# Letting two token ranges take turns by single matmuls, by threes and by twos in three of a down projection's seven products

## The chip, the cores and the metric

One core of one Trainium2 chip runs the kernel. The metric is the device time of one execution in microseconds (us). Before the change three executions took 1509.31, 1510.66 and 1514.90 us; the median is 1510.66 us. One execution was also taken with the hardware profiler, and its trace is what the views below are made of.

## The reference, cut to what matters

The kernel computes one layer of a hybrid decoder for 1024 prompt tokens and 64 sample tokens. The change lies in the last matrix product of the feed-forward part, the down projection `(gelu(a) * b) @ w_down`, with 2816 rows of weights and 1024 columns:

```python
def conv_ffn(h, w_up, conv_w, conv_b, w_down, prev):
    z = h @ w_up
    ...
    a, b = jnp.split(c, 2, axis=-1)
    return (jax.nn.gelu(a) * b) @ w_down, zp[:, T:]

def layer(...):
    ...
    f, nconv = conv_ffn(rmsnorm(x, norm_ffn), w_up, conv_w, conv_b, w_down, conv_prev)
    return x + f, nk, nv, nconv, vn
```

After it come only the residual addition and the final RMSNorm. The values are float32; the kernel reaches that accuracy with matmuls on rounded operands: each operand is split into a high part and a low part (`wh`, `wl` for weights, `th`, `tl` for tokens), and a product is the sum of three matmuls, `wh*th + wh*tl + wl*th`.

## The kernel before, in words

The down phase is the last stage. It multiplies 2x2 blocks by a scheme with seven products in place of eight. `DN_ORDER = (5, 0, 2, 4, 6, 1, 3)` is the order in which the products run; `at` counts them from 0. Each product has 11 units (`NU`), a unit being 128 rows of the contraction. A unit has its weights, 4 blocks `m` of 128 columns, and its tokens, 544 of them. The 544 tokens are two ranges `e`: a **wide** one of 288 tokens (`e == 0`) and a **narrow** one of 256 (`e == 1`).

`mm_dn(m, e, i, ws, new)` issues the three matmuls of one block and one range. The stationary operand is the block of weights, the moving operand is the range of tokens, and the output goes to `place(m, e)`: six PSUM banks (`dn`) hold the results, one bank for each of the four wide outputs, and two narrow outputs together in each of the other two banks (m = 0, 1 and m = 2, 3). So a unit is 4 x 2 x 3 = 24 matmuls, 12 wide and 12 narrow, and a product is 264. Every matmul brings its own weight load (LDWEIGHTS) along.

The loop over blocks of units: the first two and the last two units of a product go together, in two halves of two `m` each (`mp`); the seven between go one at a time with all four `m`. Within each the range `e` is the outer loop, then the units `x`, then `m`, then the three matmuls. So a single unit issues its 12 wide matmuls and then its 12 narrow ones.

When the last two units of a product are done, `take` adds each of the eight outputs from PSUM to the residual tile `x` in SBUF on VectorE (DVE, L1750). The next product may write to a bank only when that bank's takes are done. A first write with `start` clears the whole bank, and only the products at 0, 1 and 5 start anew; the others go on adding.

The operands are made ahead: SyncE (SP) issues the loads of raw weights (`wraw`, `a`) and raw tokens (`traw`); ScalarE (ACT) rounds to the high part (L40), DVE subtracts to get the low part (L41), and in some products DVE also adds two blocks of weights first (L443, L447). `units` asks for weights two units ahead and tokens some units ahead. The instructions go to the engines' queues in an order that the framework's scheduler makes of the program; the kernel has no table of times.

Of the kernel before, what the change touches and what calls it, by code (L numbers as in the profile page):

```python
# [34 lines left out]
def layer(tc, a):  # L35
# [11 lines left out]
    with ExitStack() as top:  # L47
# [310 lines left out]
        with ExitStack() as ph1:  # L358
# [98 lines left out]

            for j in DN_ORDER:
                for i in range(NFF // 2):
# [530 lines left out]
            for at, (pair, gs, whole) in enumerate(seq):  # L990
# [16 lines left out]
                ws, to = [], W.used + 7  # L1007
# [518 lines left out]
        def t_upto(loads, splits):  # L1526

            for n in range(len(ts["raw"]), min(loads, 7 * (NFF // 2))):
                j, i = DN_ORDER[n // (NFF // 2)], n % (NFF // 2)
                raw = dnp["t"].tile([P, 576], F32, name="traw", bufs=4)[:, :HT]  # L1530
                nc.sync.dma_start(raw, td[i][:, T_AT[j]])
                ts["raw"].append(raw)
# [185 lines left out]
        with ExitStack() as ph3:  # L1718
            def pool3(name, bufs, **kw):
                return ph3.enter_context(tc.tile_pool(name=name, bufs=bufs, reuse_waits="tile", **kw))  # L1720
# [4 lines left out]
            def x_load(dh, th):  # L1725
                x = x1[dh, th] = xp.tile([P, 4, HT], F32, name=f"x{dh}{th}")
                for m in range(4):
                    nc.sync.dma_start(x[:, m], x1d[4 * dh + m][:, HT * th:HT * th + HT])
# [3 lines left out]
            def place(m, e):  # L1732
                b = bank[m] if e == 0 else bank[4 + m // 2]
                return b[:, 0:288] if e == 0 else b[:, 256 * (m % 2):256 * (m % 2) + 256]

            def mm_dn(m, e, i, ws, new):
                (wh, wl), (th, tl) = ws
                lo, hi = spans[e]
                for k, (u, v) in enumerate(((wh, th), (wh, tl), (wl, th))):
                    PE.matmul(place(m, e), u[:, m, :], v[:, lo:hi],  # L1740
                              start=new and i + k == 0 and (e == 0 or m % 2 == 0),
                              stop=i == NU - 1 and k == 2, skip_group_check=True)

            def take(j, m, e):

                dh, th, op = {5: (0, 0, V.tensor_add), 0: (0, 0, V.tensor_add), 2: (0, 1, V.tensor_add),
                              4: (1, 1, V.tensor_sub), 6: (1, 0, V.tensor_sub), 1: (1, 1, V.tensor_sub),
                              3: (0, 1, V.tensor_add)}[j]
                x = x1[dh, th][:, m, spans[e][0]:spans[e][1]]
                return op(x, x, place(m, e))  # L1750
# [77 lines left out]
            def units(n, count):  # L1828
                out = []
                for x in range(n, n + count):  # L1830
                    t_upto(x + 5, x + 3)
                    w = W.get(2, 3)
                    out.append((w, ts["made"][x]))
                return out
# [17 lines left out]

            for at, j in enumerate(DN_ORDER):
                new, last, n0 = j in (5, 0, 1), at == 6, at * NU
                blocks = [(0, 2), *((x, x + 1) for x in range(2, NU - 4 if last else NU - 2))]
                if not last:
                    blocks.append((NU - 2, NU))
                for lo, hi in blocks:
                    if at == 0:
                        if lo in (2, 5):  # L1860
                            later.pop(0)()
                        if lo == 8:
                            nc.sync.dma_start(a["tails"], stc)
                            ph2.close()
                            own["s2"], own["a22"] = pool3("s2", 1), pool3("a22", 1)
                            xp, lp = pool3("xp", 1), pool3("lp", 1)
                            acc += [lp.tile([P, HT], F32, name=f"acc{th}") for th in range(2)]
                            x_load(0, 0)
                    for go in hooks.get((at, lo), ()):
                        go()  # L1870
                    got = units(n0 + lo, hi - lo)
                    for mp in range(2) if hi - lo == 2 else (0,):
                        for e in range(2):
                            for x in range(lo, hi):
                                for m in range(2 * mp, 2 * mp + 2) if hi - lo == 2 else range(4):
                                    mm_dn(m, e, x, got[x - lo], new)
                        if hi == NU:
                            for m in (2 * mp, 2 * mp + 1):
                                for e in range(2):
                                    take(j, m, e)  # L1880
            got = units(7 * NU - 4, 4)
            for e in range(2):
                sqs = []
                for m in range(4):
                    for x in range(4):
                        mm_dn(m, e, NU - 4 + x, got[x], False)
                    if e and m == 0:
                        last_scale(0, range(4))
                        fin[2] = fin_rms(1, 0, last)
                    elif e and m == 1:  # L1890
                        rb = fin_rb(*fin[2])
                        last_mul(0, 0, rb, 0, 4)
                    for m in (m - 1, m) if m % 2 and e else () if e else (m,):
                        taken = take(3, m, e)
                        sqs.append(square(0, 1, m, e, False, m < 3 - e))
                    if e and m == 1:
                        last_scale(1, (0, 1))
                last = sqs[3 - e:]
# [14 lines left out]

NSTG, FEW, NPRE = 4, 3, 2
DN_ORDER = (5, 0, 2, 4, 6, 1, 3)
T_AT = {5: 0, 3: 1, 0: 2, 4: 3, 1: 4, 2: 5, 6: 6}
OUTS = dict(y=(KD, P, T), kp=(P, 2, P), vp=(P, 256), ksn=(P, 2, NS), vsn=(8, 8, 256),
            ks=(8, 120, 256), vso=(8, 120, 256), tails=(P, 44, 9, 2), gvs=(NS, GW))
# [82 lines left out]
```

## Time and profile before

| | |
|---|---|
| three executions | 1509.31, 1510.66, 1514.90 us; median 1510.66 us |
| the profiled execution, its own time | 1509.93 us |
| its span, first to last instruction | 1508.2 us |
| granted TensorE clock, mean | 0.998 |
| DVE busy | 1158.7 us (77%) |
| ACT busy | 825.9 us (55%) |
| POOL busy | 265.8 us (18%) |
| DMA | 286.70 MB, mean 190 GB/s |

Engines: PE is TensorE's matmuls, PEld its weight loads, which run beside the matmuls; DVE is VectorE, ACT is ScalarE, POOL is GpSimd, SP is SyncE. In the timeline a row is: start in us, duration in us, engine, line, operation, output and inputs by the program's names, shape, count, and in brackets the idle time before it with what ended it. A matmul's duration overlaps with the next matmuls; what a matmul costs in a stream is the distance from its start to the next start, called its **pitch** here. The table of windows gives the busy time and number of instructions of each engine in a stretch, then the granted clock, the share of the DMA engines that was busy, and GB/s.

### The profile page before, as it was taken

Reading aid. Unit: us, or ns where it says so; the run is one execution under the profiler, and the core shown is the slowest. Engines: PE = TensorE matmul, PEld = TensorE weight load, DVE = VectorE, ACT = ScalarE, POOL = GpSimd, SP = SyncE. Lnnn points to the kernel's source line nnn. Section 1 sums busy time; section 2 is a strip of 40 time slices with the busy share of each in tenths; the row PEclk is TensorE's granted clock in tenths of the full one; section 3 lists DMA queues with packets and bytes.
Section 4 is the critical chain, followed back from the end, with each engine's and each line's share of the span. In section 5 each row is a group of like instructions: output and inputs, shape, how many; then the busy total and the mean of one; then the engine's idle time right before and its main releaser. Section 6 shows DMA issues by size and latency. Waiting matters only on the chain.

```text
span 1508.2 us, 31375 instructions
## 1 busy us (share of the span) xinstructions
PE 1493.7 (99%) x12190; PEld 1481.7 (98%) x12190; DVE 1158.7 (77%) x1909; ACT 825.9 (55%) x1755; POOL 265.8 (18%) x422
## 2 busy tenths in 40 slices
PE   9999999999999999999999999999999999999997
PEld 9999999999999999999999999999999999999997
DVE  6896778756645995989668888898899888785685
ACT  6665764544543774874434555555555556453463
POOL 0000012200120331530222322322132122000002
PEclk9999999999999999999999999999999999999999
DMA  8452457637749757849978333332233226973453
GB/s 289 157 188 112 179 177 265 228 126 271 243 167 333 249 181 224 254 160 322 342 257 282 129 115 122 117 117 107 98 136 109 91 74 219 367 259 97 123 183 133
DMA packets 137508, 286.70 MB, mean 190 GB/s; under 512 B 15248, under 2 KB 44368, under 8 KB 137360
## 3 DMA queue, kind: packets, MB, share of 16 engines
q1 hardware_dynamic: 132352, 279.97, 55.2%
q10 hardware_dynamic: 5008, 4.73, 0.9%
q8 instruction: 96, 1.57, 0.4%
q14 instruction: 52, 0.43, 0.1%
HBM read 195.76 MB, written 90.85 MB: 190 GB/s over the span
## 4 chain that ended last, share of the span: by engine, by line
PE 76%; DVE 5%; ACT 2%; issue 1%; DMA 1%; POOL 0%; DVEq 0%; ACTq 0%; POOLq 0%
PE st L300 41%; PE dn L1740 15%; PE mm L240 14%; PE sc L1233 1%; PE mx L841 1%; PE po L1294 1%; ACT s L1256 1%; DVE s L1259 1%; DVE s L1243 1%; DVE nm L1249 1%; PE pt L1266 1%; DVE of L1305 0%; DVE wl L41 0%; DVE pl L41 0%; DMA v<-gvd 0%
## 5 line engine op out<-in xcount | busy, mean ns | idle before, releaser
L300 PE MATMUL st<-th,wh 128*128 128x256 f32 (+1 forms) x2128 | 610.6, 287 | 1.2 <-ACT ku L283 0.8
L300 PE MATMUL st<-tl,wh 128*128 128x256 f32 (+1 forms) x2128 | 608.7, 286 | 0.0
L300 PE MATMUL st<-th,wl 128*128 128x256 f32 (+1 forms) x2128 | 608.2, 286 | 0.0
L300 PEld LDWEIGHTS st<-th,wh 128*128 128x128 f32 x2128 | 399.9, 188 | 2.6 <-ACT k L281 1.2
L300 PEld LDWEIGHTS st<-th,wl 128*128 128x128 f32 x2128 | 400.3, 188 | 0.0
L300 PEld LDWEIGHTS st<-tl,wh 128*128 128x128 f32 x2128 | 399.7, 188 | 0.0
L40 ACT CAST wh<-wraw 128x512 fp32r<-128x512 f32 (+2 forms) x204 | 139.4, 694 | 99.7 <-PE st L300 35.3
L41 DVE TENSOR_TENSOR wl<-wraw,wh 128x512 fp32r<-128x512 f32 (+2 forms) x204 | 158.5, 790 | 40.2 <-ACT wh L40 38.3
L1740 PE MATMUL dn<-th,wh 128*128 128x288 f32 (+1 forms) x616 | 176.7, 287 | 0.0
L1740 PE MATMUL dn<-tl,wh 128*128 128x288 f32 (+1 forms) x616 | 176.2, 286 | 0.0
L1740 PE MATMUL dn<-th,wl 128*128 128x288 f32 (+1 forms) x616 | 175.1, 284 | 0.0
L40 ACT CAST wh<-ws 128x512 fp32r<-128x512 f32 x160 | 98.1, 622 | 99.8 <-PE st L300 65.5
L41 DVE TENSOR_TENSOR wl<-ws,wh 128x512 fp32r<-128x512 f32 x160 | 111.1, 707 | 44.1 <-ACT wh L40 42.1
L1740 PEld LDWEIGHTS dn<-th,wl 128*128 128x128 f32 x616 | 115.8, 188 | 0.0
L1740 PEld LDWEIGHTS dn<-tl,wh 128*128 128x128 f32 x616 | 115.7, 188 | 0.0
L1740 PEld LDWEIGHTS dn<-th,wh 128*128 128x128 f32 x616 | 115.6, 188 | 0.0
L288 POOL TENSOR_TENSOR z<-ku,k 128x256 f32<-128x256 f32 (+1 forms) x32 | 29.5, 926 | 316.7 <-ACT ku L283 315.4
L41 DVE TENSOR_TENSOR tl<-traw,th 128x544 fp32r<-128x544 f32 (+1 forms) x85 | 61.4, 730 | 22.9 <-ACT th L40 22.8
L40 ACT CAST th<-traw 128x544 fp32r<-128x544 f32 (+1 forms) x85 | 53.8, 642 | 43.9 <-PE dn L1740 28.6
L240 PE MATMUL mm<-s,wh 128*128 128x256 f32 (+1 forms) x384 | 76.7, 294 | 0.0
L531 PE MATMUL st<-w2h,th 128*128 128x256 f32 x308 | 74.5, 283 | 0.2 <-DVE w2l L165 0.2
L240 PE MATMUL mm<-oh,wh 128*128 128x256 f32 (+1 forms) x256 | 73.5, 288 | 0.2
(300 smaller groups left out, 3157.9 us busy)
## 6 DMA issues: line engine op xcount, KB each, us to landing
wraw<-wt SPq DMA_DIRECT2D x133, 512.0 KB
traw<-td SPq DMA_DIRECT2D x77, 272.0 KB
td<-za SPq DMA_DIRECT2D x22, 544.0 KB
wraw<-wt SPq DMA_DIRECT2D x35, 256.0 KB
upd<-hl SPq DMA_DIRECT2D x14, 512.0 KB
td<-t SPq DMA_DIRECT2D x11, 544.0 KB
qd<-q SPq DMA_DIRECT2D x8, 576.0 KB
q<-qd SPq DMA_DIRECT2D x8, 576.0 KB
```

Of the source, the lines that this page charges most:

```text
L40: S.copy(hi, src)
L41: V.tensor_sub(lo, src, hi.bitcast(F32))
L240: PE.matmul(ps[:, lo:lo + c1 - c0], u[:, k, :], v[:, c0:c1], start=(clear and k == 0 and i == 0), stop=(k == nk - 1 and i == 2), skip_grou ...
L288: op(to, pick(x, to, lo, hi), pick(y, to, lo, hi))
L300: PE.matmul(ps, u[:, kk, :], v, start=first and kk + i == 0, stop=kk == 3 and i == 2, skip_group_check=True)
L531: PE.matmul(ps, u, v[:, k, :], start=k + i == 0, stop=k == KD - 1 and i == 2)
L841: PE.matmul(ps[:, P * i:P * i + P], vn[:, i], late["wst"][:, c, :], start=True, stop=True)
L1233: PE.matmul(ps[:, h, o0:256], q, kst[kv][:, e, k0:cur + P], start=e == 0, stop=e == 1)
L1243: V.copy_predicated(s[:, :, 0:P], late["mprev"].to_broadcast([P, 4, P]), ps[:, :, 0:P])
L1249: V.tensor_reduce(nm, s, AX.X, ALU.max, negate=True)
L1256: S.activation(s[:, h], s[:, h], AF.Exp, bias=nm[:, h:h + 1], accum_out=dn[:, h:h + 1])
L1740: PE.matmul(place(m, e), u[:, m, :], v[:, lo:hi], start=new and i + k == 0 and (e == 0 or m % 2 == 0), stop=i == NU - 1 and k == 2, skip_g ...
```

## The change

A table `TURNS` says for the products at 1, 2 and 3 how the two ranges take turns; the other four products are as before. `mm_dn` gets an argument `ks`, the subset of its three matmuls to issue.

```diff
-            def mm_dn(m, e, i, ws, new):
+            def mm_dn(m, e, i, ws, new, ks=range(3)):
                 (wh, wl), (th, tl) = ws
                 lo, hi = spans[e]
                 for k, (u, v) in enumerate(((wh, th), (wh, tl), (wl, th))):
+                    if k not in ks:
+                        continue
                     PE.matmul(place(m, e), u[:, m, :], v[:, lo:hi],
...
                     for mp in range(2) if hi - lo == 2 else (0,):
-                        for e in range(2):
+                        turn = TURNS.get(at)
+                        for e in range(1 if turn else 2):
                             for x in range(lo, hi):
                                 for m in range(2 * mp, 2 * mp + 2) if hi - lo == 2 else range(4):
-                                    mm_dn(m, e, x, got[x - lo], new)
+                                    for k, d in turn or ((range(3), e),):
+                                        mm_dn(m, d, x, got[x - lo], new, k)
...
+TURNS = {1: [((k,), e) for k in range(3) for e in range(2)],
+         2: [(range(3), e) for e in range(2)],
+         3: [((k,), e ^ (k % 2)) for k in range(3) for e in range(2)]}
```

The same 264 matmuls run in each product, each with its own weight load; only their order differs. With W for a wide matmul and N for a narrow one, a block `m` of a unit now reads W N W N W N at 1 (singles), W W W N N N at 2 (threes), and W N N W W N at 3 (twos, with a single at each end). Within a product the order goes from wide to narrow 11 times before, and 132, 44 and 88 times now; consecutive matmuls write to different banks 61 times before, and 263, 87 and 175 times now.

TensorE, the first matmuls of the product at 1, before (names with their numbers: `dn_16951` and `dn_16952` are the wide outputs of m = 0 and 1, `dn_16955` the bank of the narrow outputs of m = 0 and 1, `th_17339` the first unit's tokens and `th_17351` the second's; in brackets the engines whose semaphore the instruction waits for):

```order
L1740 MATMUL dn_16951<-th_17339,wh_17309 128x288 [waits DVE_49,Activation_49]
L1740 MATMUL dn_16951<-tl_17340,wh_17309 128x288
L1740 MATMUL dn_16951<-th_17339,wl_17310 128x288
L1740 MATMUL dn_16952<-th_17339,wh_17309 128x288 [waits DVE_49]
L1740 MATMUL dn_16952<-tl_17340,wh_17309 128x288
L1740 MATMUL dn_16952<-th_17339,wl_17310 128x288
L1740 MATMUL dn_16951<-th_17351,wh_17357 128x288 [waits Activation_49]
L1740 MATMUL dn_16951<-tl_17352,wh_17357 128x288
L1740 MATMUL dn_16951<-th_17351,wl_17358 128x288
L1740 MATMUL dn_16952<-th_17351,wh_17357 128x288
L1740 MATMUL dn_16952<-tl_17352,wh_17357 128x288
L1740 MATMUL dn_16952<-th_17351,wl_17358 128x288
```

The same place with the change:

```order
L1742 MATMUL dn_16951<-th_17339,wh_17309 128x288 [waits DVE_49,Activation_49]
L1742 MATMUL dn_16955<-th_17339,wh_17309 128x256 [waits DVE_49]
L1742 MATMUL dn_16951<-tl_17340,wh_17309 128x288
L1742 MATMUL dn_16955<-tl_17340,wh_17309 128x256
L1742 MATMUL dn_16951<-th_17339,wl_17310 128x288
L1742 MATMUL dn_16955<-th_17339,wl_17310 128x256
L1742 MATMUL dn_16952<-th_17339,wh_17309 128x288
L1742 MATMUL dn_16955<-th_17339,wh_17309 128x256
```

The first narrow matmul, with its wait for DVE's takes out of the shared bank `dn_16955`, was the 13th matmul of the product and is now the second; the second unit's weights and tokens were first needed at the 7th matmul and are now first needed at the 13th.

VectorE, the end of the product at 1, as a piece of the difference (L1750 and L1752 are `take`; L447 adds weights for a later unit, L41 makes low parts):

```order
 L41 TENSOR_TENSOR tl<-traw,th 128x544
-L1750 TENSOR_TENSOR x_17296<-x_17296,dn 128x288 x2
+L447 TENSOR_TENSOR s_17922<-s_17501,a_17858 128x512
+L1752 TENSOR_TENSOR x_17296<-x_17296,dn 128x288
 L41 TENSOR_TENSOR wl<-s_17860,wh 128x512
-L1750 TENSOR_TENSOR x_17296<-x_17296,dn 128x256 x2
-L447 TENSOR_TENSOR s_17922<-s_17501,a_17858 128x512
-L1750 TENSOR_TENSOR x_17296<-x_17296,dn 128x288 x2
+L1752 TENSOR_TENSOR x_17296<-x_17296,dn 128x256
+L1752 TENSOR_TENSOR x_17296<-x_17296,dn 128x288
+L1752 TENSOR_TENSOR x_17296<-x_17296,dn 128x256
```

The addition for a later unit now stands ahead of the takes, and the takes of the wide and narrow outputs alternate. SyncE's order is the same but for line numbers; ACT's order differs in a few neighbouring rounding and squaring steps.

## The prediction

> **What bounds the kernel now.** The page comes first: how busy each engine is, and the granted clock in 40 slices. Then the end of the chain of waits in order of time (start, us, what).
>
> ```profile
> span 1508.2 us, 31375 instructions
> ...
> PE 1493.7 (99%) x12190; PEld 1481.7 (98%) x12190; DVE 1158.7 (77%) x1909; ACT 825.9 (55%) x1755; POOL 265.8 (18%) x422
> ...
> PEclk9999999999999999999999999999999999999999
> ```
>
> ```profile
> 1267.10 185.64 PE dn L1740 x1512
> ```
>
> TensorE is busy nearly all the time at full clock, and the chain runs through the matmuls of the down phase in one piece of 185.64 us. A time on PE there is a time of the kernel. Next the table of windows, one window for each of the products at 1, 2, 3 and, for comparison, 4 (length, busy PE, PEld, DVE, ACT and POOL with counts, clock, DMA share, GB/s):
>
> ```profile
> 1299.35:1331.77 32.42, 32.42 (x267) 32.42 (x265) 27.95 (x50) 16.67 (x30) 0.00 (x0) 1.00 0.96 346
> 1331.77:1364.18 32.41, 32.41 (x266) 32.41 (x265) 25.84 (x48) 14.53 (x29) 0.00 (x0) 1.00 0.66 212
> 1364.18:1396.59 32.41, 32.41 (x266) 32.41 (x265) 17.93 (x31) 13.06 (x24) 0.00 (x0) 1.00 0.33 96
> 1396.59:1429.01 32.42, 32.42 (x267) 32.42 (x265) 20.80 (x37) 14.33 (x28) 0.00 (x0) 1.00 0.46 136
> ```
>
> The products take 32.41 to 32.42 us each although DVE, ACT and the DMA engines are very differently loaded in them (DMA from 0.33 to 0.96). So nothing but PE's own stream sets their length, and the reader should ask what sets the stream's pitch. The timeline of PE at the start of the product at 1 answers that.
>
> ```profile
> 1299.24 0.28 PE L1740 MATMUL dn<-th,wl 128*128 128x256 f32 x1
> 1299.35 0.29 PE L1740 MATMUL dn<-th,wh 128*128 128x288 f32 x1
> 1299.49 0.30 PE L1740 MATMUL dn<-tl,wh 128*128 128x288 f32 x1
> ...
> 1300.81 0.29 PE L1740 MATMUL dn<-th,wl 128*128 128x288 f32 x1
> 1300.94 0.28 PE L1740 MATMUL dn<-th,wh 128*128 128x256 f32 x1
> 1301.05 0.28 PE L1740 MATMUL dn<-tl,wh 128*128 128x256 f32 x1
> ...
> 1302.19 0.28 PE L1740 MATMUL dn<-th,wl 128*128 128x256 f32 x1
> 1302.30 0.29 PE L1740 MATMUL dn<-th,wh 128*128 128x288 f32 x1
> 1302.43 0.30 PE L1740 MATMUL dn<-tl,wh 128*128 128x288 f32 x1
> ```
>
> Twelve wide matmuls go from 1299.35 to 1300.94: 1.59 us, a pitch of 132.5 ns. Twelve narrow ones go from 1300.94 to 1302.30: 1.36 us, 113.3 ns. Together 2.95 us, and 11 units of that are 32.45 us, the product's length to 0.04 us. There is no gap left to remove.
>
> **The change, part by part.** Nothing is added or taken away: 264 matmuls and 264 weight loads in each product, as before. Two things move.
>
> *The turns.* Within the three products the changes from wide to narrow go from 33 to 264, and those back likewise. What a change costs can be read where the order makes one already. The last wide matmul starts at 1300.81 and the first narrow at 1300.94: 0.13 us, the wide pitch. The first narrow's own pitch is 0.11 (1300.94 to 1301.05), and the last narrow is 0.11 ahead of the first wide (1302.19 to 1302.30), whose pitch is 0.13 again. Each matmul keeps the pitch of its own width, whatever follows. So I cost the turns at **0 us**. The bounds come from the stage before, L300, where blocks of wide and narrow alternate too:
>
> ```profile
> 1201.89 0.30 PE L300 MATMUL st<-th,wl 128*128 128x288 f32 x1
> 1202.03 0.28 PE L300 MATMUL st<-th,wh 128*128 128x256 f32 x1
> ...
> 1202.50 0.28 PE L300 MATMUL st<-tl,wh 128*128 128x256 f32 x1
> ...
> 1204.77 0.29 PE L300 MATMUL st<-th,wh 128*128 128x288 f32 x1
> 1204.89 0.29 PE L300 MATMUL st<-tl,wh 128*128 128x288 f32 x1
> 1205.03 0.30 PE L300 MATMUL st<-th,wl 128*128 128x288 f32 x1
> ```
>
> Here the first four narrow matmuls after a wide one take 0.47 us (1202.03 to 1202.50), 117.5 ns each, 4.2 more than in the down phase. In the new order no narrow matmul is further than the third behind a wide one, so all 3 x 132 = 396 of them could pay that: **+1.7 us**. The first wide matmul after a narrow one has 0.12 (1204.77 to 1204.89), 12.5 ns less than the wide pitch: 264 x 12.5 ns is **-3.3 us**; but the next has 0.14 and gives most of it back, so about -1.3 us is likelier where this holds at all. I stay at 0, since the rows of the down phase itself are the nearest.
>
> Why a narrow matmul is not shorter: the weight loads.
>
> ```profile
> L1740 PEld LDWEIGHTS dn<-th,wl 128*128 128x128 f32 x616 | 115.8, 188 | 0.0
> L1740 PE MATMUL dn<-th,wh 128*128 128x256 f32 x308 | 85.3, 277 | 0.0
> ```
>
> There is one load for each matmul (616 of this kind, as many as matmuls), also where the next matmul has the same `wh`. So a longer run of the same weights, four in place of two in the singles, saves no load. If a wide matmul's 19.2 ns over the narrow pitch (132.5 - 113.3) let the loads get ahead, a narrow one behind it would need its streaming alone; scaled from the wide pitch that is 132.5 x 256/288 = 117.8 ns, more than 113.3, so there is nothing to win. The Trainium skill, "TensorE: Matmul & The Clock Gate", section "Back-to-back issue gap", says that loads and matmuls are pipelined through a window 64 deep and gives a lone matmul N/2.4 + 2.5 ns, an estimate of 109.2 ns for 256 columns; by it the turns would gain 396 x 4.1 ns = 1.6 us. The 132.5 ns measured for 288 columns, where the same formula gives 122.5, says that it doesn't hold in this stream.
>
> *The wait at the border from 0 to 1.* The first narrow matmul of the product at 1 moves from the 13th place to the second, and it waits for the takes of both narrow outputs in its bank. The timeline of DVE there, and the first use of the next unit:
>
> ```profile
> 1297.32 0.45 DVE L1750 TENSOR_TENSOR x<-x,dn 128x288 f32<-128x288 f32 x1
> 1297.69 0.69 DVE L443 TENSOR_TENSOR s<-wraw 128x512 f32<-128x512 f32 x1
> 1298.29 0.69 DVE L41 TENSOR_TENSOR wl<-wraw,wh 128x512 fp32r<-128x512 f32 x1
> 1298.89 1.11 DVE L1750 TENSOR_TENSOR x<-x,dn 128x288 f32<-128x288 f32 x3
> ...
> 1301.25 0.69 DVE L41 TENSOR_TENSOR wl<-wraw,wh 128x512 fp32r<-128x512 f32 x1
> ```
>
> ```profile
> 1305.25 0.29 PE L1740 MATMUL dn<-th,wh 128*128 128x288 f32 x1
> ```
>
> The three takes (one wide, two narrow) end at 1298.89 + 1.11 = 1300.00; the product at 0 and DVE's order up to there are unchanged, so this time stands. From a DVE result to the matmul that waits for it the chain shows 0.14 us:
>
> ```profile
> 1500.57 0.30 DVE dg L1785
> 1500.86 0.14 issue
> 1501.00 0.70 PE fs L1791 x4
> ```
>
> So the narrow matmul starts at 1300.14 in place of 1299.35 + 0.13 = 1299.48: **+0.66 us** of idle PE. Behind it in PE's queue is all the rest of the product, so the whole of it counts. If one narrow take were enough it would be about 0.33. Before, this wait was hidden behind twelve wide matmuls (1.59 us).
>
> *The other borders and DVE's new order.* The takes of a half follow its matmuls, and the next product needs a bank only after the other half, 24 matmuls or 2.95 us later. At the border from 1 to 2 DVE's rows were
>
> ```profile
> 1328.41 0.81 DVE L1750 TENSOR_TENSOR x<-x,dn 128x288 f32<-128x288 f32 x2
> 1329.14 0.69 DVE L41 TENSOR_TENSOR wl<-s,wh 128x512 fp32r<-128x512 f32 x1
> 1329.74 0.75 DVE L1750 TENSOR_TENSOR x<-x,dn 128x256 f32<-128x256 f32 x2
> ```
>
> The takes of the first half ended at 1330.49. With one addition of 0.69 us put ahead of them they end near 1331.2, and the bank is needed at 1331.77 + 0.66 + 0.13 = 1332.6: 1.4 us of cover, **0 us**. Of two more DVE steps of 0.69 (1.38 us) in the way nothing would show either. Operands are made further ahead: the low weights at 1301.25 end at 1301.94 and are first used at 1305.25, 3.3 us later, and the second unit of the product at 1 is needed later than before. SP's order is unchanged, so the loads at DMA share 0.96 aren't moved.
>
> **The sum.** The profiled execution's 1509.93 us (span 1508.2 and 1.73 around it) + 0 + 0.66 = 1510.6. The runs' median lies 0.73 us above it, so on its scale the forecast is **1511.3 us**.
>
> **The rivals.** All on the median's scale; 0.5% is 7.55 us, about what a measurement of this kernel can tell from no change.
>
> *Each turn has the transient of L300*: 1511.3 + 1.7 = 1513.0. For it: the same engine, widths and clock. Against it: in the down phase the narrow pitch is 0.11 from the first matmul on.
>
> *Turns shorten the wide matmuls*: 1511.3 - 1.3 = 1510.0, at the end 1508.0. For it is the 0.12 at 1204.77, against it the 0.13 at 1302.30.
>
> *A narrow matmul behind a wide one takes the wide pitch*: 264 x 19.2 ns = 5.1 us, 1516.4, still within 0.5%. Against it speaks the row at 1300.94.
>
> *A change of bank costs time* (slower). Consecutive matmuls change bank 525 times in the three products, 183 before, 342 more. From (7.55 - 0.66)/342 = 20 ns a change it is slower by over 0.5%. If a change kept the next matmul from overlapping, the price would be the whole duration, 277 - 113 = 164 ns: 56 us, 1567. Against it: a bank changes after every third wide matmul now, and 12 of them still have 132.5 ns on average.
>
> *The clock falls* (slower). If the turns made PE idle in small pieces, the granted clock could fall; at half the clock in all three products their 97.2 us (3 x 32.41) would double: 1608. Against it: the clock is 1.00 in windows with 61 bank changes each, and busy PE equals the window. The Trainium skill, in the same page's section "A second HAM failure mode: psum-queue depth-cycling", tells of a kernel whose cycling through PSUM banks did this; here the trace doesn't agree so far.
>
> **How the numbers follow.** Forecast 0.55, transient 0.22, shorter wide matmuls 0.12, wide pitch 0.05, cost of a bank change 0.03, fallen clock 0.01, and 0.02 for a gain of over 7.55 us, which would need 10 ns off each of the 792 matmuls and for which no row speaks. So faster 0.02, same 0.94, slower 0.04. The range goes from the end of the shorter wide matmuls, 1508.0, to 1515.5, past the transient at 1513.0 by the 2.5 us that single runs scatter upward (1514.90 against 1510.66 is 4.2 for one of three); it leaves out the wide pitch and the two slower cases, 0.09 in all, and the 0.02 of a gain.
>
> **What would show it.** In the changed profile the products at 1, 2 and 3 should be 33.1, 32.4 and 32.4 us; the one at 4 is the control with 32.4. An idle of 0.66 us behind the first matmul of the product at 1 shows the wait. A pitch of narrow matmuls of 118 or 132 in place of 113 shows the second or fourth case, one of 120 or 127 for wide ones the third; a loss that grows with the bank changes (263 : 87 : 175) the last. I'm wrong if a product's length changes by over 1 us without idle time, or if a later border shows a wait.

## The result, and the profile after

Timed beside each other, 17 executions each, the kernel before has a median of 1512.33 us (1509.31 to 1514.90) and the changed one 1514.72 us (1511.67 to 1516.67). The ratio is 1.0019 with a 95% interval of 1.0012 to 1.0026. That is 2.9 us more (1.8 to 3.9): far within 0.5%, but not nothing.

The profiled execution of the changed kernel took 1511.67 us. From its page:

```profile
span 1510.0 us, 31373 instructions
...
PE 1496.1 (99%) x12190; PEld 1484.8 (98%) x12190; DVE 1159.9 (77%) x1909; ACT 827.3 (55%) x1755; POOL 264.9 (18%) x422
...
PEclk9999999999999999999999999999999999999999
```

The matmuls are as many as before and the clock is full as before, but PE is busy 2.4 us longer. (The two profiled spans, 1508.2 and 1510.0 us, differ by less than the products below do, mostly because the product at 1 began 1.17 us earlier in this execution, at 1298.18 in place of 1299.35.) The table of windows (length, busy time and count of PE, PEld, DVE, ACT, POOL, clock, DMA share, GB/s) gives the products at 1, 2, 3, 4 and 5:

```profile
1298.18:1331.18 33.00, 33.00 (x266) 33.00 (x265) 26.88 (x47) 16.38 (x30) 0.00 (x0) 1.00 0.90 318
1331.18:1364.32 33.14, 33.14 (x267) 33.14 (x265) 25.32 (x47) 14.83 (x28) 0.00 (x0) 1.00 0.63 205
1364.32:1397.19 32.87, 32.87 (x267) 32.87 (x265) 17.65 (x32) 12.60 (x23) 0.00 (x0) 1.00 0.35 95
1397.19:1430.12 32.93, 32.93 (x267) 32.93 (x265) 20.88 (x39) 14.30 (x27) 0.00 (x0) 1.00 0.46 134
1430.12:1463.94 33.82, 33.82 (x276) 33.82 (x275) 27.35 (x54) 20.60 (x39) 0.00 (x0) 1.00 0.60 185
```

The products at 1 to 4 took 32.41 to 32.42 us before. The row of the product at 5, not shown so far, is in the profile of before

```profile
1429.01:1462.32 33.31, 33.31 (x276) 33.31 (x275) 27.27 (x53) 20.50 (x39) 0.00 (x0) 1.00 0.60 187
```

So the five windows are longer by 0.58, 0.73, 0.46, 0.51 and 0.51 us, 2.8 us together. Two things are to be seen. PE is busy over the whole of each window, so the time isn't in waits. And the products at 4 and 5, **which the change doesn't touch**, lose 0.51 us each, about as much as those it does.

The timeline of PE in the product at 4 says how. Twelve narrow matmuls run from the first row to the fourth, with the order of before:

```profile
1398.77 0.28 PE L1742 MATMUL dn<-th,wh 128*128 128x256 f32 x1
1398.89 0.28 PE L1742 MATMUL dn<-tl,wh 128*128 128x256 f32 x1
...
1400.07 0.28 PE L1742 MATMUL dn<-th,wl 128*128 128x256 f32 x1
1400.18 0.30 PE L1742 MATMUL dn<-th,wh 128*128 128x288 f32 x1
```

From 1398.77 to 1400.18 are 1.41 us, a pitch of 117.5 ns where the product at 1 had 113.3 before. I call these the **long** and the **short** pitch of narrow matmuls. 132 narrow matmuls times 4.2 ns are 0.55 us, the product's loss of 0.51 to 0.04 us.

In the singles (a row x2 is a wide matmul and the narrow one behind it, under the wide one's name):

```profile
1299.18 0.41 PE L1742 MATMUL dn<-tl,wh 128*128 128x288 f32 x2
...
1303.18 0.41 PE L1742 MATMUL dn<-th,wl 128*128 128x288 f32 x2
```

16 pairs take 4.00 us, 250 ns each, where a wide and a narrow pitch of before are 132.5 + 113.3 = 245.8 ns. And the wait at the border from 0 to 1 isn't there in this execution. DVE's timeline:

```profile
1295.28 0.69 DVE L41 TENSOR_TENSOR wl<-wraw,wh 128x512 fp32r<-128x512 f32 x1
1295.88 1.11 DVE L1752 TENSOR_TENSOR x<-x,dn 128x288 f32<-128x288 f32 x3
```

The takes end at 1296.99, 1.2 us before the product at 1 starts (1298.18). In the execution of before they ended 0.65 us after its start.

Was the long pitch there in before at all? Yes, in several places; two of them are shown. In the last product of before, small matmuls `fs` of the final RMSNorm stand between the others; behind them (timeline of PE)

```profile
1468.32 0.80 PE L1791 MATMUL fs<-dg,c_ones 96*128 96x96 f32 x6
...
1470.57 0.28 PE L1740 MATMUL dn<-th,wh 128*128 128x256 f32 x1
...
1471.99 0.60 PE L1791 MATMUL fs<-dg,c_ones 128*128 128x128 f32 x4
```

the twelve narrow ones from 1470.57 to 1471.99 have 118 ns. And in the first stage, narrow matmuls only (L531), the window from 50 to 112 us of before holds 529 in 62.00 us, 117 ns each (with those at both edges counted):

```profile
50.00:112.00 62.00, 62.00 (x529) 62.00 (x529) 59.12 (x113) 37.20 (x76) 0.00 (x0) 1.00 0.54 174
```

So the theory: the stream has **two steady pitches**, the turns move it to the long one, and it keeps that pitch over product borders until something moves it back. The rivals: each product's loss comes from its own order or its own neighbours (the products at 4 and 5 then need another cause), each bank change costs a little, or the loss is a scatter of executions.

### The profile page after: what moved, and what is told of

It reads as the page before. It is cut to its first block, busy times and chain, and to the rows that moved or that the text cites. A ratio compares the mean times of both kernels' runs of the same rounds, so it can differ in the third digit from the quotient of the medians.

```text
span 1510.0 us, 31373 instructions
## 1 busy us (share of the span) xinstructions
PE 1496.1 (99%) x12190; PEld 1484.8 (98%) x12190; DVE 1159.9 (77%) x1909; ACT 827.3 (55%) x1755; POOL 264.9 (18%) x422
## 4 chain that ended last, share of the span: by engine, by line
PE 76%; DVE 5%; ACT 1%; issue 1%; DMA 1%; POOL 0%; DVEq 0%; ACTq 0%; POOLq 0%
PE st L300 41%; PE dn L1742 15%; PE mm L240 15%; PE sc L1233 1%; PE mx L841 1%; PE po L1294 1%; ACT s L1256 1%; DVE s L1259 1%; DVE s L1243 1%; DVE nm L1249 1%; PE pt L1266 1%; DVE wl L41 0%; DVE pl L41 0%; DMA vnd<-v 0%; DVE of L1305 0%
## 5 line engine op out<-in xcount | busy, mean ns | idle before, releaser
L300 PE MATMUL st<-th,wh 128*128 128x256 f32 (+1 forms) x2128 | 610.3, 287 | 0.6 <-ACT ku L283 0.3
L300 PE MATMUL st<-tl,wh 128*128 128x256 f32 (+1 forms) x2128 | 608.4, 286 | 0.0
L300 PE MATMUL st<-th,wl 128*128 128x256 f32 (+1 forms) x2128 | 608.0, 286 | 0.0
L300 PEld LDWEIGHTS st<-th,wh 128*128 128x128 f32 x2128 | 399.9, 188 | 1.8 <-ACT k L281 0.9
L300 PEld LDWEIGHTS st<-th,wl 128*128 128x128 f32 x2128 | 400.2, 188 | 0.0
L300 PEld LDWEIGHTS st<-tl,wh 128*128 128x128 f32 x2128 | 399.7, 188 | 0.0
L41 DVE TENSOR_TENSOR wl<-wraw,wh 128x512 fp32r<-128x512 f32 (+2 forms) x204 | 158.7, 790 | 37.2 <-ACT wh L40 35.4
L1742 PE MATMUL dn<-th,wh 128*128 128x288 f32 (+1 forms) x616 | 163.2, 288 | 0.0
L1742 PE MATMUL dn<-tl,wh 128*128 128x288 f32 (+1 forms) x616 | 162.5, 287 | 0.0
L1742 PE MATMUL dn<-th,wl 128*128 128x288 f32 (+1 forms) x616 | 161.9, 286 | 0.0
L41 DVE TENSOR_TENSOR wl<-ws,wh 128x512 fp32r<-128x512 f32 x160 | 110.1, 700 | 46.9 <-ACT wh L40 44.8
L1742 PEld LDWEIGHTS dn<-th,wl 128*128 128x128 f32 x616 | 110.2, 188 | 0.0
L1742 PEld LDWEIGHTS dn<-th,wh 128*128 128x128 f32 x616 | 110.1, 189 | 0.0
L1742 PEld LDWEIGHTS dn<-tl,wh 128*128 128x128 f32 x616 | 109.7, 188 | 0.0
L41 DVE TENSOR_TENSOR tl<-traw,th 128x544 fp32r<-128x544 f32 (+1 forms) x85 | 61.7, 731 | 26.6 <-ACT th L40 26.5
L531 PE MATMUL st<-w2h,th 128*128 128x256 f32 x308 | 75.4, 286 | 0.8 <-ACT w2h L40 0.8
L240 PE MATMUL mm<-ol,wh 128*128 128x256 f32 (+1 forms) x256 | 73.7, 288 | 0.0
```

Of the source, the lines that this page charges most:

```text
L41: V.tensor_sub(lo, src, hi.bitcast(F32))
L240: PE.matmul(ps[:, lo:lo + c1 - c0], u[:, k, :], v[:, c0:c1], start=(clear and k == 0 and i == 0), stop=(k == nk - 1 and i == 2), skip_grou ...
L300: PE.matmul(ps, u[:, kk, :], v, start=first and kk + i == 0, stop=kk == 3 and i == 2, skip_group_check=True)
L531: PE.matmul(ps, u, v[:, k, :], start=k + i == 0, stop=k == KD - 1 and i == 2)
L1742: PE.matmul(place(m, e), u[:, m, :], v[:, lo:hi], start=new and i + k == 0 and (e == 0 or m % 2 == 0), stop=i == NU - 1 and k == 2, skip_g ...
```

## The experiments

Lengths of the products in every profile, in us, from windows like those above; **bold** is a product whose ranges take turns. Where a wait stands in the product at 1 it is given in brackets beside the length that contains it, as the distance from the start of one matmul to the start of the one that waits, less its usual 0.13. The matmul behind one that has waited starts some 0.1 us late as well, which is in the length; in the change's second execution that 0.1 us is all there is. The window at 4 of the column pokes begins behind them.

| kernel | at 1 (its wait) | at 2 | at 3 | at 4 | at 5 |
|---|---|---|---|---|---|
| before | 32.42 | 32.41 | 32.41 | 32.42 | 33.31 |
| the change | **33.00** (0) | **33.14** | **32.87** | 32.93 | 33.82 |
| singles alone | **34.72** (1.61) | 32.42 | 32.41 | 32.41 | 33.32 |
| threes alone | 32.41 | **32.56** | 32.41 | 32.41 | 33.32 |
| twos alone | 32.41 | 32.41 | **32.85** | 32.41 | 33.32 |
| change and column pokes at 4 | **33.00** (0) | **33.13** | **32.87** | 33.01 | 33.83 |
| pokes at 1, no turns | 33.11 | 32.41 | 32.41 | 32.41 | 33.32 |
| threes then twos | 32.41 | **32.56** | **32.85** | 32.41 | 33.31 |
| singles then threes | **34.03** (0.92) | **33.13** | 32.92 | 32.93 | 33.83 |
| change and square pokes at 4 | **33.00** (0) | **33.13** | **32.87** | 33.24 | 33.32 |
| pokes in the first stage, no turns | 33.81 (0.76) | 32.93 | 32.93 | 32.92 | 33.83 |
| the change, again | **33.11** (0.1) | **32.57** | **32.85** | 32.41 | 33.32 |
| threes then twos, timed | 32.41 | **32.56** | **32.85** | 32.41 | 33.32 |
| singles alone, timed | **33.00** (0) | 32.42 | 32.41 | 32.41 | 33.32 |

**One product alone.** Each kernel keeps one entry of the table, as here for the singles.

```diff
-TURNS = {1: [((k,), e) for k in range(3) for e in range(2)],
-         2: [(range(3), e) for e in range(2)],
-         3: [((k,), e ^ (k % 2)) for k in range(3) for e in range(2)]}
+TURNS = {1: [((k,), e) for k in range(3) for e in range(2)]}
```

> Turns by single matmuls at product 1 only; all other products in the order of before. Theory (carried state: the stream has two steady pitches for narrow matmuls, 113.3 and 117.8 ns, and the turns leave it in the slow one, where it stays): product 1 is 33.0 us, and the unturned products 2, 3 and 4 are 32.9 us each in place of 32.41, so about 2.6 us more than before through product 5. Rival (a cost of each turn, and something else slows 4 and 5): product 1 is 33.0 us, products 2 to 4 are 32.41.

Time 1512.07 us, 1512.94 for before beside it. The windows of the products at 1 and 2:

```profile
1298.67:1333.39 34.72, 33.28 (x267) 33.06 (x265) 29.76 (x53) 17.57 (x31) 0.00 (x0) 1.00 0.89 320
1333.39:1365.81 32.42, 32.42 (x266) 32.42 (x265) 25.16 (x47) 14.01 (x27) 0.00 (x0) 1.00 0.67 213
```

This time PE is busy 1.44 us less than the window is long. Its timeline, and DVE's there:

```profile
1298.67 0.29 PE L1742 MATMUL dn<-th,wh 128*128 128x288 f32 x1
1300.41 0.39 PE L1742 MATMUL dn<-th,wh 128*128 128x256 f32 x1 [1.44 <-DVE x L1752]
```

```profile
1296.58 0.45 DVE L1752 TENSOR_TENSOR x<-x,dn 128x288 f32<-128x288 f32 x1
1297.97 0.69 DVE L443 TENSOR_TENSOR s<-wraw 128x512 f32<-128x512 f32 x1 [0.95 <-DMA wraw<-wt]
1298.63 0.69 DVE L41 TENSOR_TENSOR wl<-wraw,wh 128x512 fp32r<-128x512 f32 x1
1299.24 1.11 DVE L1752 TENSOR_TENSOR x<-x,dn 128x288 f32<-128x288 f32 x3
```

Here is the wait of the prediction, behind the first matmul and released by `take`; the theory's 32.9 us at 2 to 4 did not come. Ahead of the last three takes in DVE's queue stands an addition that itself waits 0.95 us for a load of raw weights; so the takes end at 1300.35 and the narrow matmul starts at 1300.41. Without its 1.61 us the product has 33.11, and 33.00 without the late start behind the wait, as in the change. But it hands nothing on: 32.42 at 2.

> Turns by threes at product 2 only. Carried state: product 1 is 32.41, product 2 33.1, products 3 and 4 32.9 us though their order is that of before. Cost of each turn: 2 is 33.1, 3 and 4 are 32.41.

Time 1509.53 us (before 1512.94). The windows of the products at 2 and 3:

```profile
1331.08:1363.64 32.56, 32.56 (x266) 32.56 (x265) 26.36 (x49) 15.76 (x30) 0.00 (x0) 1.00 0.69 221
1363.64:1396.05 32.41, 32.41 (x266) 32.41 (x265) 17.78 (x32) 12.26 (x22) 0.00 (x0) 1.00 0.34 96
```

The same order that had 33.14 behind the singles has 32.56 behind an ordinary product. The threes' own cost is 0.15 us; the other 0.57 came from outside. Here too the theory expected more, 33.1 at 2 and 32.9 behind it.

> Turns by twos at product 3 only. Carried state: products 1 and 2 are 32.41, 3 is 32.9, 4 is 32.9 and 5 33.8 us as in the whole change. Cost of each turn: 3 is 32.9, 4 is 32.41, 5 33.3.

Time 1510.72 us (before 1512.94). The windows of the products at 3 and 4:

```profile
1364.51:1397.36 32.85, 32.85 (x267) 32.85 (x265) 17.84 (x31) 13.38 (x25) 0.00 (x0) 1.00 0.34 95
1397.36:1429.77 32.41, 32.41 (x266) 32.41 (x265) 20.77 (x38) 14.18 (x27) 0.00 (x0) 1.00 0.46 136
```

0.44 of their own, nearly as in the change (0.46), and nothing handed on, for the third time against the theory: what is carried needs more than one turned product. The three own costs together are 0.59 + 0.15 + 0.44 = 1.18 us; the change paid 2.8. So 1.6 us were **carried**: 0.57 at 2 and 0.51 at 4 and at 5.

**Pokes of single columns.** Small matmuls that nobody reads (pokes) are put in front of the product at 4, behind all the turns.

```diff
+            def poke_columns():
+                ps = psl.tile([P, 512], F32, name="fs", bufs=2)
+                for i in range(2):
+                    PE.matmul(ps[:, 320 + i:321 + i], ident, ones[:, 0:1], start=i == 0, stop=True,
...
+            hooks[4, 0] = [poke_columns]
```

> The whole change, and ahead of product 4 two more matmuls of one column each into a spare bank (about 0.3 us of stream), like those that stand ahead of product 6. Carried state: the stream can leave the slow pitch there, as it does ahead of product 6; then product 4 has narrow matmuls of 113.3 ns and 32.4 us beside the 0.3, and 5 33.3 us, about 0.7 us less in all. Rival (4 and 5 are slowed by operands, banks or DVE's order): both stay at 32.9 and 33.8. If the pitch stays 117.8 here, it is open whether the poke was of the wrong kind.

Time 1514.43 us (before 1512.94). A miss for the hoped-for end of the long pitch, and it doesn't tell the theory from its rival. The pokes didn't move the pitch: the product at 5 keeps the long one, in the window

```profile
1431.55:1465.38 33.83, 33.83 (x277) 33.83 (x275) 27.45 (x54) 20.75 (x40) 0.00 (x0) 1.00 0.59 185
```

**Square pokes without turns.** If small matmuls set the long pitch in the last product, they should do it in an untouched one too. On the kernel before:

```diff
+            def poke_squares():
+                ps = psl.tile([P, 512], F32, name="fs", bufs=2)
+                for i in range(3):
+                    PE.matmul(ps[:, i * 96:i * 96 + 96], ones[0:96], ident[0:96, 0:96], start=True, stop=True)
+
+            hooks[1, 2] = [poke_squares]
```

> The kernel before, without turns, and ahead of the third unit of product 1 three more float32 matmuls of 96 columns into a spare bank, like those that stand in product 6, behind which the narrow matmuls took 117.8 ns for two units. Carried state: without any turn the narrow pitch goes to 117.8 and products 2, 3 and 4 take 32.9 us each; an ordinary order is then as slow behind a poke as it was behind the turns. Rival (only the turned order or something it left in DVE's queue or the banks slows the stream): 2, 3 and 4 stay at 32.41 and only product 1 is longer by the poke, 0.6 us.

Time 1511.52 us (before 1511.02). A miss. The product at 1 grew by 0.69 us, nearly all of it the pokes' own time, and the one at 2 is as ever:

```profile
1332.57:1364.98 32.41, 32.41 (x266) 32.41 (x265) 25.07 (x46) 13.98 (x27) 0.00 (x0) 1.00 0.64 213
```

**Pairs of products.** One kernel keeps the threes and the twos, one the singles and the threes.

> Turns at products 2 (threes) and 3 (twos), product 1 as before. Carried state: the threes start from the fast pitch and take 32.56 us as when alone, not 33.13 as in the whole change; the twos take 32.85 and product 4 is 32.4, so 0.6 us in all. Cost that belongs to the order alone: the threes take 33.1 us here as they do behind the singles.

Time 1511.71 us (before 1511.02). The products at 2, 3 and 4 have 32.56, 32.85 and 32.41: each its own cost, nothing carried.

> Turns at products 1 (singles) and 2 (threes), 3 as before. Carried state: the threes behind the singles take 33.1 us, 0.57 more than alone; what product 3 does after them isn't certain: 32.9 if the threes hand the slow pitch on, 32.41 if not. Cost that belongs to the order alone: 32.56 as alone. Beside this, at the border from 0 to 1 a wait of 0 to 1.7 us for the takes, by when DVE gets to them.

Time 1517.53 us (before 1511.02). The windows of the products at 2, 3 and 4, of which only the first takes turns:

```profile
1336.63:1369.76 33.13, 33.13 (x267) 33.13 (x265) 25.41 (x47) 14.82 (x28) 0.00 (x0) 1.00 0.64 208
1369.76:1402.68 32.92, 32.92 (x266) 32.92 (x265) 17.75 (x32) 12.29 (x22) 0.00 (x0) 1.00 0.33 95
1402.68:1435.61 32.93, 32.93 (x266) 32.93 (x265) 20.72 (x38) 14.43 (x28) 0.00 (x0) 1.00 0.45 134
```

Threes behind singles have the long pitch, and they hand it to three ordinary products in a row (0.51 us each). The twos aren't needed for it. The product at 1 has a wait of 0.92 us in this execution.

**Square pokes behind the turns.** The pokes of three squares, in the changed kernel, ahead of the third unit of the product at 4 (`hooks[4, 2].insert(0, poke_squares)`).

> The whole change, and ahead of the third unit of product 4 the three matmuls of 96 columns. The two matmuls of one column didn't move the narrow pitch. Carried state: this other poke may or may not; if it does, the rest of product 4 and product 5 have 113.3 ns and 5 takes 33.3 us. Rival (slowed by operands, banks or DVE's order): 117.8 ns and 33.8 us whatever the poke.

Time 1513.42 us (before 1511.02). A hit, the strongest evidence that something is carried. The timeline of PE, with the poke (three matmuls of the program, six records in the trace), the narrow matmuls of the next unit, and those of the unit behind it:

```profile
1405.15 0.81 PE L1858 MATMUL fs<-c_ident,c_ones 96*128 96x96 f32 x6
...
1407.40 0.28 PE L1742 MATMUL dn<-th,wh 128*128 128x256 f32 x1
...
1408.82 0.30 PE L1742 MATMUL dn<-th,wh 128*128 128x288 f32 x1
...
1410.40 0.28 PE L1742 MATMUL dn<-th,wh 128*128 128x256 f32 x1
...
1410.87 0.28 PE L1742 MATMUL dn<-tl,wh 128*128 128x256 f32 x1
...
1411.78 0.29 PE L1742 MATMUL dn<-th,wh 128*128 128x288 f32 x1
```

The first twelve narrow ones still take 1.42 us (118 ns). In the next unit the first four take 0.47 us, the last eight 0.91 us (114 ns): the pitch is short again, and the product at 5 has its length of before (33.31) to 0.01:

```profile
1432.40:1465.72 33.32, 33.32 (x277) 33.32 (x275) 26.41 (x51) 19.70 (x37) 0.00 (x0) 1.00 0.58 181
```

The operands, DMA traffic and orders of that product are those of the change, where it has 33.82.

**Pokes in the first stage.** If the long pitch there is the same carried state, pokes might end it and win time. On the kernel before, ahead of four groups of tokens of L531:

```diff
+                    if i == 0:
+                        for _ in range({(0, "gv2"): 1, (1, "v"): 2, (1, "gv2"): 3, (1, "gv0"): 1}.get((g, key), 0)):
+                            PE.matmul(ps[:, 0:96], ones[0:96], ones[0:96, 0:96], start=True, stop=True,
...
```

> The kernel before, and in the first stage (L531, where all 530 narrow matmuls from 50 to 112 us take 117.8 ns) one, two, three and one float32 matmuls of 96 columns ahead of four of the six groups of tokens. Carried state: it isn't a property of the down phase; a poke that moves the state takes the group behind it to 113.3 ns and it stays until the next poke; if the first does so for good the stage is 2.3 us shorter less 0.2 to 0.6 us for each poke. Rival (117.8 ns is what this stage's operands allow): 117.8 ns in all groups, and the kernel is about 1.5 us longer by the pokes.

Time 1515.64 us (before 1511.62). A miss: with the pokes in it the window still holds 530 matmuls in 62.00 us.

```profile
50.00:112.00 62.00, 62.00 (x530) 62.00 (x529) 59.55 (x113) 37.68 (x77) 0.00 (x0) 1.00 0.54 174
```

Whether that stage allows only the long pitch or the pokes weren't of the right kind stays open. But the kernel is 4.0 us longer, where 1.5 were expected, and its products at 1 to 5, which have no turns here, are together 3.45 us longer than in the profile of before. The timeline of PE at the start of the product at 1, and the windows of the products at 1 and 2:

```profile
1301.82 0.29 PE L1744 MATMUL dn<-th,wl 128*128 128x288 f32 x1
1302.71 0.40 PE L1744 MATMUL dn<-th,wh 128*128 128x288 f32 x1 [0.61 <-DVE x L1754]
```

```profile
1301.55:1335.36 33.81, 33.20 (x267) 32.97 (x265) 28.79 (x53) 16.39 (x29) 0.00 (x0) 1.00 0.90 326
1335.36:1368.29 32.93, 32.93 (x267) 32.93 (x266) 26.12 (x48) 14.85 (x29) 0.00 (x0) 1.00 0.67 214
```

The fourth matmul of the product at 1, in the order of before, waits for a take (L1754 is `take` here). Behind that wait the narrow matmuls have the long pitch, and the products at 2 to 4 take 32.92 to 32.93 us and the one at 5 33.83, as the untouched products of the change do. The pokes didn't hand it on directly, since the product at 0 between them still has the short pitch and 32.41 us. So the long pitch **needs no turns**: here it follows a wait, and the order of before doesn't rule it out.

**The change once more,** unaltered.

> The changed kernel itself, once more. Carried state: products 1 to 5 again 33.0, 33.1, 32.9, 32.9 and 33.8 us, since the order alone leads the stream there; only the wait at the border from 0 to 1 (0 to 1.7 us, by when DVE gets to the takes) differs from run to run. Rival (the state is chance): 4 and 5 are 32.4 and 33.3 in some runs.

Time 1512.14 us (before 1511.62). A miss that limits the theory. The windows of the products at 1 to 4:

```profile
1299.77:1332.88 33.11, 33.11 (x267) 33.06 (x265) 28.20 (x50) 17.57 (x31) 0.00 (x0) 1.00 0.91 327
1332.88:1365.45 32.57, 32.57 (x267) 32.57 (x265) 25.25 (x47) 14.81 (x28) 0.00 (x0) 1.00 0.67 214
1365.45:1398.30 32.85, 32.85 (x266) 32.85 (x265) 17.68 (x32) 12.59 (x23) 0.00 (x0) 1.00 0.34 95
1398.30:1430.71 32.41, 32.41 (x266) 32.41 (x265) 20.68 (x38) 14.18 (x27) 0.00 (x0) 1.00 0.48 136
```

The same program on another execution pays the own costs and 0.1 us of wait only. So with this order the long pitch can be handed on, but needn't be.

**The same traces to the nanosecond.** The traces keep each start to 1 ns, which the timeline rounds to 10. In the ordinary order the wide pitches of a stream at the short pitch (the short state) go round in six steps (132, 136, 128, 134, 131, 132 ns) with narrow ones of 113 and 114; at the long pitch (the long state) they go round in four (127, 135, 133, 132) with narrow ones of 117 to 119. Twelve wide matmuls are whole rounds of either, so a steady stream comes out of each unit as it went in; that fits with a state that is carried.

Over the fourteen profiles, 179 stretches of twelve wide and then twelve narrow matmuls in the down phase had the round of four. In 17 the last two wide pitches were 127 (or 126) and 135, and the narrow ones fell to the short pitch after three; in the other 162 they didn't. Fourteen of the 17 stand at one place of the last product, once in each profile; the other three are the second unit behind the square pokes and the product behind the singles in both kernels with singles alone. In the singles the pairs go round in four as well, and where threes follow, the last wide pitch of the singles is 132 in the four profiles that hand the long pitch on and 133, one step earlier in the round, in the one that doesn't. So what goes with the handing on is the step at which the next order begins. That is seen in the traces; no run here put a stream on a chosen step.

**Two of them timed,** in five rounds each.

> Turns by threes and by twos, no singles, now timed over many executions. The two products cost 0.15 and 0.44 us of their own by the profiles, no later product pays and no border waits, so the ratio to the kernel before should be 1.0004 (0.6 us of 1512). If the whole change's loss (ratio 1.0019) lay in the turns as such, each by its number, threes and twos would have half of it, 1.001.

Median 1512.42 us of 11 executions against 1510.95 of 21 before; ratio 1.0012, 95% interval 1.0002 to 1.0022 (0.3 to 3.3 us). The expected 1.0004 and the rival's 1.001 both lie within: not settled. Its profile, of one of the 11, again shows nothing carried.

> Turns by singles at product 1 alone, timed. The product costs 0.6 us of its own, the wait at the border from 0 to 1 adds 0 to 1.7 us by execution (0.4 on average in the six profiles with singles), and where the slow pitch is handed on to product 2 up to 2.1 us more. If nothing is handed on, the ratio is 1.0007; if in most executions it is, 1.0015 or more. If the wait is usual in timed executions, 1.001 without any handing on; the profile of this run says which of the two it had.

Median 1511.28 us of 11 against the same 1510.95; ratio 1.0004, interval 0.9996 to 1.0013. The products add 0.59 us in its profile, with nothing handed on and no wait. The expected 1.0007 fits; 1.001 lies within too, 1.0015 doesn't.

## Why the prediction was right and wrong

The forecast was +0.66 us on a before of 1510.66; measured are +2.9 (1.8 to 3.9) on a before whose median came to 1512.33 with more executions. So of the 3.4 us by which 1511.3 fell short of 1514.72, 1.7 are the base's scatter (1512.33 - 1510.66) and 1.7 the change itself (by the medians +2.39 in place of +0.66). "Within 0.5%" was right, and so was that PE's own stream sets the time. The median lies inside the range of 1508.0 to 1515.5, but not by the mechanism that was forecast: the upper end was set by a rival and by the scatter of single runs, and half of the distance is scatter of the base, so that it held is in part luck.

**The step that failed: "So I cost the turns at 0 us".** In the profiles they cost 1.2 us in their own products and, where the long pitch is handed on, 1.6 us more. I took the rows of the down phase as the nearest; these show only one of the two pitches. "Each matmul keeps the pitch of its own width, whatever follows" was read from a stream that was steady in the short one. The other was in the same trace, in the first stage and behind the `fs` matmuls of the last product, and in the four matmuls of L300 at 117.5 ns. Those four were a transient of one border, as the prediction says, since the trace has 113 and 114 ns behind them; but their number was that of the long pitch. The sign that the prediction named, narrow matmuls at 118, did come.

**The transient as a rival** was nearest in kind. Taken alone, singles, threes and twos lose 0.59, 0.15 and 0.44 us; they add 132 - 11 = 121, 33 and 77 changes from wide to narrow, which is 4.9, 4.5 and 5.7 ns for a change. That even price is a quotient, not a mechanism: by the starts in the traces the narrow matmuls of singles, threes and twos average 120.0, 114.3 and 118.2 ns (113.3 in the short state), and the wide ones 130.0, 132.3 and 130.7 (132.2). So the 396 narrow matmuls take 1.6 to 1.7 us more, close to the rival's 1.7, though not evenly, and the wide ones 0.5 us less. What the rival lacked is the carried part: it was to be paid in the turned products only, and "the one at 4 is the control with 32.4" was wrong. A neighbour in the same stream is no control where something is carried. That threes lose 0.15 or 0.72 us by what ran before them is what no cost by changes can give.

**"This time stands", of the wait,** was wrong, though its mechanism is right. DVE reaches these takes at another time from execution to execution: with singles alone an addition ahead of them waited 0.95 us for a load. In the seven profiles with singles the wait is 0, 1.61, 0, 0.92, 0, 0.1 and 0 us, a mean of 0.4. Forecast was 0.66 from one execution.

**Do the parts make up the whole?** Of four profiles with all three turns, three handed the long pitch on, which adds 2.8 us to the five products (the two with pokes have more or less of it behind these), and one didn't, which adds 1.3 with its wait. That is a mean of (3 x 2.8 + 1.3)/4 = 2.4 us; with a mean wait of 0.4 in place of the four's own, some 2.8. The measured 2.9 (1.8 to 3.9) agrees, and no other cause is needed. But this takes the kernel before as always in the short state, as in its one profile; the pokes in the first stage show that its order can be in the long one, and how often either kernel is so in executions without a profile isn't known.

**The other borders and operands** cost nothing, as forecast: in the changed profile PE is busy throughout the windows of the products at 2 to 5, at a DMA share of up to 0.63.

**The other rivals.** *A change of bank costs time*: the own losses divided by the 202, 26 and 114 added bank changes are 2.9, 5.8 and 3.9 ns each, a less even price than by changes from wide to narrow; the runs don't tell these two apart further. But behind singles the same 87 bank changes lose 0.72 us, and the product at 4 loses 0.51 with no added one, so neither price gives the whole, and the 20 ns from which it would be slower by over 0.5% is ruled out. *The clock falls*: it is 1.00 in every window. The Trainium skill, "TensorE: Matmul & The Clock Gate", section "A second HAM failure mode: psum-queue depth-cycling", tells of a clock that oscillates when cycling through banks leaves PE idle in small pieces; here 263 bank changes in 33.0 us came with PE busy all the time and a clock of 1.00, so those idle pieces didn't come and the run doesn't test what they would do. *Shorter wide matmuls*: those of the singles and twos are indeed 2.2 and 1.5 ns shorter, but the narrow ones lose more, and a pair of the singles has 250 ns, not less than 245.8. *The wide pitch for narrow matmuls* would have made a pair 265 ns.

On the pitch itself, the formula for a lone matmul in the Trainium skill, same page, section "Back-to-back issue gap", gives one price for a width, an estimate of 109.2 ns here. The traces show 113.3 and 117.5 to 118 for the same 256 columns in a stream, so the formula gives neither the level nor which of the two holds.

**Open:** what in the engine makes the two rounds, and whether the step at a border decides alone if the long pitch is handed on. Of five profiles in which threes follow singles four had the long pitch at 2; of two in which an ordinary product follows singles none had. The length of the wait doesn't decide it (handed on after 0.92 and after 0, not after 0.1). The threes or ordinary products at 2 to 4 that had the long pitch always handed it on up to the product at 5, unless square pokes ended it; the column pokes didn't. At the border to the last product, where four column records of the final norm stand, the pitch was short again (113 ns from 1465.61 in the changed profile). No version here beats the kernel before: even threes alone, whose one time was 1509.53 us, have a product of 32.56 in place of 32.41.

## What to carry to other kernels

Before a new order of matmuls is costed at nothing, look through the whole trace for the same shape at another pitch: if there are two steady values, the order or a wait may move the stream from one to the other, and the cost then covers what follows in the same stream. Compare lengths stage by stage, in the untouched stages too, and take one changed part alone before a loss is put down to it. Where something ahead of it in its queue waits for a load, a wait that is read from a single execution needn't come again.

## What the runs showed that was not expected

- Narrow matmuls (256 columns) in the ordinary order, in a stream without gaps and at full clock, run steadily at 113.3 or at 117.5 to 118 ns, over hundreds of matmuls and over product borders. It is 4%, and 0.5 us for an ordinary product.
- In a kernel without turns a wait for a take at the start of the product at 1 was followed by the long pitch through five products.
- The same program had the long pitch at 4 and 5 in one execution (32.93 and 33.82 us) and not in another (32.41 and 33.32).
- Three small matmuls (96 columns, six records) ended the long pitch in the second unit behind them in one place; in an untouched product the same pokes left the short one as it was; and behind six `fs` records of 96 columns in the last product of before the pitch is the long one.
